# A float32 trunk kernel: the last projection's first 704 tokens by seven products for each two feature tiles, and the convolution's first four products in a written order

## The chip, the cores and the metric

One core of one Trainium2 chip runs the whole program as one launch. The metric is device time in microseconds (us) of one execution, taken as the median of several. TensorE (PE) multiplies, with its weight loads shown apart (PEld); VectorE (DVE), ScalarE (ACT) and GpSimd (POOL) do the elementwise work; SyncE (SP) issues all DMAs.

## The reference, cut to what matters

The reference is a two-layer encoder for 1024 tokens with 1024 features, all in float32. Two stages of it matter here: the gated convolution's input projection, and the second layer's attention into 256 memory tokens with its output projection, behind which only the final norm stands.

```python
def conv_mixer(xn, w_in, conv_w, conv_b, w_out):
    gb, gc, u, gate = jnp.split(xn @ w_in, 4, axis=-1)
    ...

def memory_cross_attention(xn, memn, wq, wkv, wo):
    ...
    o = jnp.einsum('bhsm,bmhd->bshd', p, v).reshape(b, s, D_MODEL)
    return o @ wo

    ...
        x = x + memory_cross_attention(rmsnorm(x, c_norm[i]), rmsnorm(mem, c_mem_norm[i]),
                                       c_wq[i], c_wkv[i], c_wo[i])
    return rmsnorm(x, final_norm)
```

## The kernel before

**Tiling.** Activations lie transposed: eight feature tiles of 128 partitions, each with 1024 tokens. A float32 operand is split into a high part (a cast on ACT, line 214) and a low part (a subtraction on DVE, line 215), and `mm3` multiplies with three matmuls (lines 198 to 200). `dense` makes one feature tile of a projection: 8 input tiles times 3 matmuls for each token part.

**Weights.** `Weights` holds a queue of units in a fixed order (the list `order` at the end of `kernel`). A plain unit is one tile of 1024 columns, split by lines 89 and 90 into two pages, `whi` and `wlo`. A pair entry loads two feature tiles and yields seven units, the left factors A11, S1, A12, S2, S3, S4, A22 of 512 columns each; S1 to S4 are sums and differences that POOL makes (lines 101 to 104; for the first pair DVE makes them), and each factor is split into one page `wf` (lines 113 and 114). There are six pages in all, so the cast of a unit waits until the product with the unit six places ahead is done. Raw weights have two buffers, `wraw`.

**Seven products.** `strassen` multiplies two feature tiles (two by four blocks of 128 input features) with two token halves by seven half-size products in place of eight: left factors times the right factors B11, T1, B21, T2, T3, B22, T4. The convolution's input projection runs so, with 16 pairs of feature tiles and halves of 512 tokens; its right factors are made by `right_factors` while the projection before it runs. `norm_half` for the second token half is issued behind the first pair's first product (`conv_in`).

**The last stages.** `cross` runs four heads; for each, two `dense` calls make the query tiles, then `cross_unit` handles token half 0 and half 1: scores (`pssc`), row maxima (line 851), exponentials (856), normalising (860), transposes (866), and the product with V into `psa`, which goes to an output. For the last head the six output tiles of the earlier heads are split at once (`split_k`), and `last_proj` then runs `dense` over three token parts, 384, 320 and 320 wide, eight feature tiles each. Line 352 adds the old x, `squares` adds up the squares, `norm_soon` makes the norm of a part with two matmuls (lines 286 and 287), and line 360 scales and the result is written out.

**Order.** The program is written in sequence, but a scheduler reorders each engine's instructions by its own timing model; `issue_after` holds instructions back until a named one was issued. Each engine then runs its instructions strictly in the order so fixed, and an instruction whose input is not ready holds up all behind it on its engine.

## Time and profile before

| | us |
|---|---|
| three runs, median (lowest to highest) | 1465.87 (1464.1 to 1466.63) |
| the profiled execution, its own time | 1467.48 |
| span of its trace, first to last instruction | 1465.7 |
| PE busy in the span | 1437.8 (98%) |
| DVE busy, ACT busy, POOL busy | 920.4, 641.4, 259.7 |
| HBM read and written | 124.90 MB and 27.26 MB |

The table's busy times are sums over the span. Matmuls overlap one another in the trace, so a start-to-start distance, not the duration of one, tells what a matmul costs PE. All times below are us from the start of the span.

### The profile page before, as it was taken

The numbers are of one execution on the slowest core, as the hardware profiler recorded it, in microseconds if no ns is written. First come the engines' busy times: TensorE is split into PE (matmuls) and PEld (weight loads), VectorE is DVE, ScalarE is ACT, GpSimd is POOL, SyncE is SP. The second block draws the span as 40 slices with busy tenths as digits, with TensorE's granted clock in tenths as the row PEclk, the third lists the DMA queues.
The fourth block names the chain that finished last, engine by engine and source line by source line (L and its number), as shares of the span: only waits on it lengthen the run. The fifth ranks groups of instructions, "written<-read, shape, count | busy, mean of one in ns | idle before, by whom it ended". The sixth has DMA issues, their size and how long they took to land.

```text
span 1465.7 us, 18632 instructions
## 1 busy us (share of the span) xinstructions
PE 1437.8 (98%) x7128; PEld 1210.9 (83%) x7128; DVE 920.4 (63%) x1368; ACT 641.4 (44%) x1160; POOL 259.7 (18%) x174
## 2 busy tenths in 40 slices
PE   7999999999999999999999999999999999999996
PEld 5888888888888888888887788888888888888996
DVE  7656666677657346446469777777776337446555
ACT  6534653343346244335466533333353325335554
POOL 2300101334220210000112433333310220000221
PEclk9999999999999999999999999999999999999999
DMA  6442223322355421013763111112235532101464
GB/s 218 132 172 71 87 73 101 101 58 72 101 202 193 152 86 44 30 43 130 220 211 119 54 58 58 52 50 58 58 124 188 192 118 79 34 30 40 134 208 152
DMA packets 54216, 157.56 MB, mean 108 GB/s; under 512 B 6640, under 2 KB 17008, under 8 KB 53360
## 3 DMA queue, kind: packets, MB, share of 16 engines
q1 hardware_dynamic: 54128, 156.38, 33.3%
q8 instruction: 56, 0.92, 0.3%
q14 instruction: 32, 0.26, 0.1%
HBM read 124.90 MB, written 27.26 MB: 104 GB/s over the span
## 4 chain that ended last, share of the span: by engine, by line
PE 91%; DVE 4%; DMA 2%; ACT 1%; issue 1%; POOL 0%; SPq 0%; DVEq 0%; ACTq 0%; POOLq 0%
PE psd L198 19%; PE psd L200 19%; PE psd L199 19%; PE pssc L198 6%; PE pssc L199 6%; PE pssc L200 6%; PE psa L199 4%; PE psa L198 4%; PE psa L200 4%; PE pssc L385 1%; DMA wraw<-w_o 1%; PE psa L415 1%; PE psa L866 1%; DVE xnew L360 1%; DVE T L215 0%
## 5 line engine op out<-in xcount | busy, mean ns | idle before, releaser
L198 PE MATMUL psd<-xh,whi 128*128 128x512 f32 (+2 forms) x1096 | 413.4, 381 | 8.8 <-ACT whi L89 7.6
L200 PE MATMUL psd<-xh,wlo 128*128 128x512 f32 (+2 forms) x1096 | 415.3, 380 | 0.9 <-DVE wlo L90 0.9
L199 PE MATMUL psd<-xl,whi 128*128 128x512 f32 (+2 forms) x1096 | 415.9, 380 | 0.0
L198 PEld LDWEIGHTS psd<-xh,whi 128*128 128x128 f32 x1096 | 206.3, 189 | 46.2 <-ACT whi L89 8.5
L200 PEld LDWEIGHTS psd<-xh,wlo 128*128 128x128 f32 x1096 | 206.6, 188 | 36.5 <-DVE wlo L90 1.6
L199 PEld LDWEIGHTS psd<-xl,whi 128*128 128x128 f32 x1096 | 206.6, 189 | 34.0
L89 ACT CAST whi<-wraw 128x1024 fp32r<-128x1024 f32 (+1 forms) x131 | 136.9, 1046 | 204.9 <-PE psd L199 133.9
L90 DVE TENSOR_TENSOR wlo<-wraw,whi 128x1024 fp32r<-128x1024 f32 (+1 forms) x131 | 163.6, 1251 | 71.4 <-ACT whi L89 71.1
L258 POOL TENSOR_TENSOR ssq<-ssq,xold 128x512 f32<-128x512 f32 (+2 forms) x42 | 60.5, 1440 | 415.2 <-ACT xold L256 360.0
L305 DVE TENSOR_TENSOR xnew<-psd,xold 128x512 f32<-128x512 f32 x32 | 21.8, 690 | 93.6 <-PE psd L200 93.6
L113 ACT CAST wf<-ws 128x512 fp32r<-128x512 f32 x64 | 39.6, 622 | 82.2 <-PE pssc L200 33.2
L198 PE MATMUL pssc<-T,wf 128*128 128x512 f32 x192 | 74.8, 390 | 0.6 <-ACT T L214 0.6
L200 PE MATMUL pssc<-T,wf 128*128 128x512 f32 x192 | 74.7, 389 | 0.0
L199 PE MATMUL pssc<-T,wf 128*128 128x512 f32 x192 | 74.7, 389 | 0.0
L258 POOL TENSOR_TENSOR ssq<-ssq,sq 128x512 f32<-128x512 f32 x12 | 19.8, 1650 | 244.6 <-ACT sq L256 244.6
L214 ACT CAST Th<-psa 128x512 fp32r<-128x512 f32 (+1 forms) x62 | 34.5, 590 | 64.2 <-PE psa L415 34.5
L114 DVE TENSOR_TENSOR wf<-ws,wf 128x512 fp32r<-128x512 f32 x64 | 56.0, 877 | 9.8 <-ACT wf L113 8.9
L215 DVE TENSOR_TENSOR Tl<-psa,Th 128x512 fp32r<-128x512 f32 (+1 forms) x62 | 41.7, 687 | 25.9 <-ACT Th L214 25.8
L101 POOL TENSOR_TENSOR ws<-wraw 128x512 f32<-128x512 f32 x15 | 22.1, 1471 | 193.4 <-DMA wraw<-w_o_in 172.4
L292 DVE TENSOR_TENSOR q<-psd,R 128x512 f32<-128x512 f32 x32 | 22.1, 691 | 53.8 <-PE psd L200 53.7
L256 ACT ACTIVATE xold<-xnew 128x512 f32<-128x512 f32 (+2 forms) x49 | 27.7, 567 | 56.2 <-DVE xnew L305 33.4
L113 ACT CAST wf<-wraw 128x512 fp32r<-128x512 f32 x48 | 29.9, 624 | 50.3 <-PE pssc L200 36.9
(316 smaller groups left out, 2997.9 us busy)
## 6 DMA issues: line engine op xcount, KB each, us to landing
wraw<-w_o SPq DMA_DIRECT2D x40, 512.0 KB, 3.8
wraw<-w_o_in SPq DMA_DIRECT2D x32, 512.0 KB, 3.6
wraw<-w_e_in SPq DMA_DIRECT2D x25, 512.0 KB, 3.9
wraw<-w_k SPq DMA_DIRECT2D x16, 512.0 KB, 4.0
mn<-memn SPq DMA_DIRECT2D x16, 512.0 KB, 4.6
wraw<-w_v SPq DMA_DIRECT2D x16, 512.0 KB, 4.6
xold<-x SPq DMA_DIRECT2D x16, 512.0 KB, 5.2
x<-xnew SPq DMA_DIRECT2D x16, 512.0 KB, 2.6
```

The source lines that it names most:

```text
L89: self.nc.scalar.copy(hi[:, c], raw[:, c])
L90: self.nc.vector.tensor_tensor(lo[:, c], raw[:, c], hi[:, c].bitcast(F32), op=ALU.subtract)
L101: tt(F["S1"], F["A21"], F["A22"], op=ALU.add)
L113: self.nc.scalar.copy(hi, src)
L114: self.nc.vector.tensor_tensor(lo, src, hi.bitcast(F32), op=ALU.subtract)
L198: mm(o, ah, bh, start=first, stop=False, skip_group_check=more)
L199: mm(o, ah, bl, start=False, stop=False, skip_group_check=more)
L200: self.last_mm = mm(o, al, bh, start=False, stop=last, skip_group_check=more)
L214: self.nc.scalar.copy(hi, src)
L215: return (eng or self.nc.vector).tensor_tensor(lo, src, hi.bitcast(F32), op=ALU.subtract)
L256: nc.scalar.activation(sq, x, AF.Square)
L258: eng.tensor_tensor(self.ssq[:, a:b], self.ssq[:, a:b], sq, op=ALU.add)
```

## The change

The last projection's first 704 tokens are no longer two dense parts, but four pairs of feature tiles by `strassen` with token halves of 352; the last 320 tokens stay dense. Its right factors are made by the new `last_factors` from the attention's outputs, in two steps: B11, T1 and B21 behind token half 0 of the last head (B21 needs half 0 of that head, tiles 6 and 7), and T2, T3, B22, T4 and the remaining 320 tokens behind half 1 (each of these four needs columns that half 1 writes, for two of its four input tiles). The first pair uses three `psd` banks and its products are issued in written order, behind the last query projection (`last_q`); the later pairs are held back until the first pair's fourth product. The last weights are loaded as four pairs and eight plain tiles, where before each of the eight was loaded three times. The old x comes in pieces of 352 tokens, 16 of them, and 320. The norms of the two halves are issued behind the first and the second of the dense tiles.

In `strassen` the `yield` moves from behind the first product to behind the fourth, and for the convolution's first pair each product's twelve matmuls are issued behind the product before. So `norm_half` of the second token half comes behind the fourth product.

```diff
+    def last_factors(self, x):
+        xh, xl = ([self.buf(tag, "f", dt=F32R) for _ in range(KT)] for tag in ("xh", "xl"))
+        T2, T3 = ([self.buf("e", "f", (P, 4, H), F32R) for _ in range(2)] for _ in range(2))
+        T4 = [self.buf("T", "f", (P, 2, H), F32R) for _ in range(3)]
+        t4 = [self.buf("t", "f", (P, L), F32R) for _ in range(2)]
+        B11, B12, B21, B22 = ([x[4 * i + k][:, j * L : j * L + L] for k in range(4)]
+                              for i in range(2) for j in range(2))
...
+        for k in range(4):
+            split("B11", k, B11[k])
+        for k in range(4):
+            sub(B11[k], B12[k], B11[k])
+            split("T1", k, B11[k])
+        for k in range(4):
+            split("B21", k, B21[k])
+        yield
+        for k in range(4):
+            sub(B11[k], B22[k], B11[k])
+            split("T2", k, B11[k])
+        for k in range(4):
+            sub(B12[k], B22[k], B12[k])
+            split("T3", k, B12[k])
+        for k in range(4):
+            split("B22", k, B22[k])
+        for k in range(4):
+            sub(B21[k], B21[k], B11[k])
+            split("T4", k, B21[k])
+        for k in range(KT):
+            self.split(xh[k][:, 2 * L :], xl[k][:, 2 * L :], x[k][:, 2 * L :])
+        yield out, list(zip(xh, xl))
...
-        for a, b in parts:
             for m in range(KT):
-                old = self.buf("v", "xold", (P, b - a))
-                nc.sync.dma_start(old, x_old[m][:, a:b])
...
+        def pair(p):
+            olds = {(i, j): old(2 * p + i, half[j]) for i, j in ((0, 0), (1, 1), (0, 1), (1, 0))}
+
+            def keep(i, j, ps):
+                t = olds[i, j]
+                nc.vector.tensor_tensor(t, ps, t, op=ALU.add)
+                return t
+
+            def out(i, j, ps, more):
+                added(2 * p + i, half[j], ps, olds[i, j] if more is None else more)
+
+            return self.strassen(B, out, keep, p == 0, L)
+
+        self.last_mm = self.last_q
+        with ExitStack() as behind:
+            for p in range(4):
+                steps = pair(p)
+                next(steps)
+                if p == 0:
+                    first = self.last_mm
+                for _ in steps:
+                    pass
+                if p == 0:
+                    behind.enter_context(self.tc.issue_after(first.ins))
+        c = slice(2 * L, S)
+        for m in range(KT):
+            t = old(m, c)
+            self.dense(ys, lambda a, b, ps: added(m, c, ps, t), ((c.start, c.stop),))
+            if m < 2:
+                with self.tc.issue_after(self.last_mm.ins):
+                    normed(half[1 - m])
+        normed(c)
...
-    def strassen(self, B, out, keep):
+    def strassen(self, B, out, keep, ordered, n=H):
         def product(ps, f, first):
             ah, al = self.w.take()
+            with self.tc.issue_after(self.last_mm.ins) if ordered else ExitStack():
+                four(ps, ah, al, f, first)
...
-        a, c, b = self.ps("sc"), self.ps("a"), self.ps("d")
+        tags = "ddd" if ordered and n < H else ("sc", "a", "d")
+        a, c, b = (self.ps(tag)[:, :n] for tag in tags)
         product(a, "B11", True)
         p1 = keep(0, 0, a)
-        yield
         product(c, "T1", True)
         p5 = keep(1, 1, c)
         product(b, "B21", True)
         out(0, 0, b, p1)
         product(a, "T2", False)
         u2 = keep(0, 1, a)
+        yield
...
-            steps = self.times(B, d, None if i % 2 else AF.Silu)
+            steps = self.times(B, d, None if i % 2 else AF.Silu, i == 0)
...
-    order += mixed("w_o_out", 1, "w_v1", 2) + tiles("w_q1", *["w_o1"] * len(LAST))
+    order += mixed("w_o_out", 1, "w_v1", 2) + tiles("w_q1")
+    o1 = tiles("w_o1")
+    order += [(o1[i], o1[i + 1], W.FACTORS) for i in range(0, len(o1), 2)] + o1
```

**At the start of the convolution, PE.** Names: `pssc_6983`, `psa_6984` and `psd_6985` are the first pair's banks, `pssc_7139`, `psa_7140` and `psd_7141` the second's; T_884 is part of T1, T_907 of T2, T_911 of T3, B_870 of B11 and B_874 of B21. In the program before, `wf_7068`, `wf_7049` and `wf_7085` are S1, A11 and A12 of the second pair, and the order behind the first pair's T2 product is:

```order
L198 MATMUL pssc_6983<-T_907_6898,wf_6908 128x512
L270 MATMUL psa_7009<-sq_928_7007,mean_dr 128x512
L198 MATMUL psa_6984<-T_884_6631,wf_6863 128x512
L199 MATMUL psa_6984<-T_884_6631,wf_6863 128x512
```

The T2 product is cut short by the norm's matmul (line 270), and only then comes the T1 product, 12 matmuls of which two stand here. In the program after, where `wf_7033` and `wf_7085` are the second pair's A11 and A12:

```order
L198 MATMUL pssc_7139<-B_873_6563,wf_7033 128x512
L199 MATMUL pssc_7139<-B_873_6563,wf_7033 128x512
L200 MATMUL pssc_7139<-B_873_6563,wf_7033 128x512
L199 MATMUL pssc_6983<-T_907_6898,wf_6908 128x512
L200 MATMUL pssc_6983<-T_907_6898,wf_6908 128x512
L198 MATMUL psd_7141<-B_874_6566,wf_7085 128x512
L199 MATMUL psd_7141<-B_874_6566,wf_7085 128x512
L198 MATMUL pssc_6983<-T_911_6946,wf_6986 128x512
```

The T1 product now runs ahead of B21 and T2, and the second pair's whole B11 product fills in between T2's matmuls; the norm's matmuls come 20 and 28 rows further on.

**The same place, ACT.** Before:

```order
L214 CAST B_918_6967<-xnew_5953 128x512
L214 CAST sq_928_7007<-ssq_84 128x512
L113 CAST wf_7068<-ws_7043 128x512
L113 CAST wf_7049<-wraw_0_7025 128x512
L701 ACT_TABLE_LOAD
L701 ACTIVATE y_923_6982<-y_923_6982 128x512
L113 CAST wf_7085<-wraw_0_7025 128x512
```

After:

```order
L793 COPY kept_7025<-psa_6984 128x512
L113 CAST wf_7033<-wraw_0_7009 128x512
L214 CAST T_907_6898<-xnew_5949 128x512
L214 CAST T_914_6955<-xnew_5949 128x512
L214 CAST B_915_6958<-xnew_5950 128x512
L214 CAST B_916_6961<-xnew_5951 128x512
L214 CAST B_917_6964<-xnew_5952 128x512
L214 CAST B_918_6967<-xnew_5953 128x512
L113 CAST wf_7052<-ws_7027 128x512
L113 CAST wf_7085<-wraw_0_7009 128x512
L793 COPY kept_7067<-pssc_6983 128x512
L214 CAST sq_932_7070<-ssq_84 128x512
```

The second pair's A11 moves ahead of the last T2 cast; its S1 (from `ws`, which POOL makes) and A12 now stand directly behind the B22 casts, and the table load with the Silu behind them.

**Behind the last head's half 1, PE.** `psa_11121` and `psa_11130` before, `psa_11152` and `psa_11160` after, are that half's products with V. Before:

```order
L199 MATMUL psa_11130<-Tl_11106,V_9221 128x512
L200 MATMUL psa_11130<-Th_11105,V_9222 128x512
L198 MATMUL psd_11259<-xh_10949,whi_11179 128x384
L199 MATMUL psd_11259<-xl_10950,whi_11179 128x384
L198 MATMUL psd_11296<-xh_10949,whi_11216 128x384
```

After, where `f_11053` holds T2 of input tiles 2 and 3, and `f_11036` is B11:

```order
L199 MATMUL psa_11160<-Tl_11137,V_9221 128x512
L200 MATMUL psa_11160<-Th_11136,V_9222 128x512
L198 MATMUL psd_11244<-f_11053,wf_10896 128x352
L199 MATMUL psd_11244<-f_11053,wf_10896 128x352
L200 MATMUL psd_11244<-f_11053,wf_10896 128x352
L198 MATMUL psd_11244<-f_11053,wf_10896 128x352
L199 MATMUL psd_11244<-f_11053,wf_10896 128x352
L200 MATMUL psd_11244<-f_11053,wf_10896 128x352
L198 MATMUL pssc_11386<-f_11036,wf_11286 128x352
```

Before, PE went on with tokens 0 to 383, which are complete; now six matmuls of T2 that need half 1 stand there, and the second pair's products behind them.

**The same place, DVE,** after (before, two subtractions of the outputs stood here, between weight splits). `q_10279`, `q_10280` are input tiles 2 and 3 and `q_10839`, `q_10840` tiles 6 and 7; `x2` marks two rows in one. Between the two pieces stand nine rows of T3, T4 and B22:

```order
L366 TENSOR_TENSOR q_10279<-q_10839,q_10279 128x352 x2
L366 TENSOR_TENSOR q_10839<-q_10839,q_10279 128x352
L366 TENSOR_TENSOR q_10280<-q_10840,q_10280 128x352 x2
L215 TENSOR_TENSOR f_11050<-q_10839,f_11050 128x352
L215 TENSOR_TENSOR f_11050<-q_10839,f_11042 128x320
```

```order
L215 TENSOR_TENSOR f_11051<-q_10840,f_11051 128x352
L215 TENSOR_TENSOR f_11051<-q_10840,f_11043 128x320
L215 TENSOR_TENSOR f_11055<-q_10279,f_11055 128x352
L215 TENSOR_TENSOR f_11058<-q_10839,f_11058 128x352
L215 TENSOR_TENSOR f_11053<-q_10280,f_11053 128x352
L215 TENSOR_TENSOR f_11055<-q_10280,f_11055 128x352
```

The low part of T2's last tile (`f_11053` from `q_10280`) is the sixteenth of DVE's instructions behind half 1's outputs.

## Rows read from the trace of the kernel before

**Rows 1.** The page: the chain's shares by engine; and one line of part 5.

```profile
PE 91%; DVE 4%; DMA 2%; ACT 1%; issue 1%; POOL 0%; SPq 0%; DVEq 0%; ACTq 0%; POOLq 0%
...
L198 PEld LDWEIGHTS psd<-xh,whi 128*128 128x128 f32 x1096 | 206.3, 189 | 46.2 <-ACT whi L89 8.5
```

**Rows 2.** PE's timeline (start, duration, instruction), last stage: scores, and the last matmul.

```profile
1345.14 0.28 PE L198 MATMUL pssc<-K,qh 128*128 128x256 f32 x1
...
1453.69 0.31 PE L200 MATMUL psd<-xh,wlo 128*128 128x320 f32 x1
```

**Rows 3.** PE's timeline: matmuls of 384 columns, 39 apart, and of 320, 56 apart.

```profile
1376.53 0.33 PE L198 MATMUL psd<-xh,whi 128*128 128x384 f32 x1
...
1383.29 0.33 PE L198 MATMUL psd<-xh,whi 128*128 128x384 f32 x1
...
1429.83 0.31 PE L199 MATMUL psd<-xl,whi 128*128 128x320 f32 x1
...
1438.04 0.31 PE L198 MATMUL psd<-xh,whi 128*128 128x320 f32 x1
```

**Rows 4.** Timelines of DVE, ACT and PE: the last head's softmax for half 0.

```profile
1351.14 0.16 DVE L854 TENSOR_SCALAR mx<-mx 128x4 f32<-128x4 f32 x1
...
1353.58 1.14 DVE L860 TENSOR_SCALAR P<-P,sm 128x256 f32<-128x256 f32 x4
...
1357.36 1.04 PE L866 MATMUL psa<-ident,P 128*128 128x128 f32 x8
...
1358.21 1.08 ACT L214 CAST Th<-psa 128x512 fp32r<-128x512 f32 x2 [4.88 <-PE psa L866]
...
1359.28 1.28 DVE L215 TENSOR_TENSOR Tl<-psa,Th 128x512 fp32r<-128x512 f32 x2
```

**Rows 5.** Timelines of DVE and ACT: instructions back to back, of 320, 512 and 384 columns.

```profile
1458.95 3.31 DVE L360 TENSOR_TENSOR xnew<-xnew,R 128x320 f32<-128x320 f32 x8
...
807.23 1.89 DVE L215 TENSOR_TENSOR B<-xnew,B 128x512 fp32r<-128x512 f32 x3
...
1370.00 0.52 ACT L254 ACTIVATE ssq<-xnew 128x384 f32<-128x384 f32 x1
1370.42 0.52 ACT L256 ACTIVATE xold<-xnew 128x384 f32<-128x384 f32 x1
```

**Rows 6.** PE's timeline at the convolution's start; idle time and its cause in brackets.

```profile
797.69 0.39 PE L198 MATMUL psd<-B,wf 128*128 128x512 f32 x1
...
803.20 0.49 PE L198 MATMUL pssc<-T,wf 128*128 128x512 f32 x1 [0.59 <-ACT T L214]
806.40 0.50 PE L270 MATMUL psa<-sq,mean_dr 128*128 128x512 f32 x1 [2.71 <-ACT sq L214]
...
815.74 0.50 PE L198 MATMUL psd<-B,wf 128*128 128x512 f32 x1 [1.49 <-ACT wf L113]
```

**Rows 7.** Windows: length, busy PE, PEld, DVE, ACT, POOL, granted clock, DMA share, GB/s.

```profile
807.65:811.06 3.41, 3.41 (x9) 2.64 (x8) 3.27 (x6) 0.00 (x0) 2.99 (x1) 0.50 0.00 0
...
823.00:1110.00 287.00, 287.00 (x1268) 237.73 (x1267) 216.97 (x268) 109.74 (x178) 79.98 (x56) 1.00 0.23 70
```

**Rows 8.** Timelines of POOL, DVE and ACT around the second pair's sums.

```profile
808.07 3.99 POOL L101 TENSOR_TENSOR ws<-wraw 128x512 f32<-128x512 f32 x1 [9.13 <-DVE B L215]
812.02 1.27 POOL L103 TENSOR_TENSOR ws<-wraw,wraw 128x512 f32<-128x512 f32 x1
...
810.24 0.69 DVE L215 TENSOR_TENSOR sq<-ssq,sq 128x512 fp32r<-128x512 f32 x1
...
812.09 0.62 ACT L113 CAST wf<-ws 128x512 fp32r<-128x512 f32 x1 [5.74 <-POOL ws L101]
812.62 0.62 ACT L113 CAST wf<-wraw 128x512 fp32r<-128x512 f32 x1
```

**Rows 9.** Timelines of POOL and DVE: one overlap where DVE gave way.

```profile
787.88 1.52 POOL L258 TENSOR_TENSOR ssq<-ssq,sq 128x512 f32<-128x512 f32 x1 [5.14 <-ACT sq L256]
...
788.17 1.78 DVE L215 TENSOR_TENSOR T<-xnew,T 128x512 fp32r<-128x512 f32 x1
```

**Rows 10.** SP's timeline, last stage: result writes ahead of a weight load.

```profile
1404.71 4.94 SPq L361 DMA_DIRECT2D out<-xnew  x8
1409.82 0.36 SPq L78 DMA_DIRECT2D wraw<-w_o  x1
```

More of the change, by code (lines that the diff above doesn't have):

```diff
@@ L339, in out_proj_halves, with split, sub @@
         return sq
[L341 to L361 removed]
+    def last_factors(self, x):
[5 more added lines that the diff above has]
+                              for i in range(2) for j in range(2))
+        out = {}
+        def split(f, k, src):
+            if f in ("T2", "T3"):
+                t = (T2 if f == "T2" else T3)[k // 2]
+                hi, lo = t[:, 2 * (k % 2), :L], t[:, 2 * (k % 2) + 1, :L]
+            elif f == "T4":
+                hi, lo = t4 if k == 3 else (T4[k][:, 0, :L], T4[k][:, 1, :L])
+            else:
+                t = (xh if f in ("B11", "T1") else xl)[k + 4 * (f in ("T1", "B22"))]
+                hi, lo = t[:, :L], t[:, L : 2 * L]
+            self.split(hi, lo, src)
+            out.setdefault(f, []).append((hi, lo))
+        def sub(to, a, b):
+            self.nc.vector.tensor_tensor(to, a, b, op=ALU.subtract)
+        for k in range(4):
[20 more added lines that the diff above has]
+        yield out, list(zip(xh, xl))
@@ L712, in out @@
                 nc.vector.tensor_tensor(c, ps, c, op=ALU.mult)
-        return self.strassen(B, out, keep)
+        return self.strassen(B, out, keep, ordered)
     def conv_in(self, B, rest):
@@ L901, in cross @@
             else:
-                ys = [self.split_k(o) for o in wait]
-                ys += [(self.buf("xh", "xh", dt=F32R), self.buf("xl", "xl", dt=F32R))
-                       for _ in range(2)]
-                out = lambda dt, c, ps: self.split(ys[6 + dt][0][:, c], ys[6 + dt][1][:, c], ps)
+                out = lambda dt, c, ps: self.nc.scalar.copy(q[dt][:, c], ps)
+                factors = self.last_factors(wait + q)
             for h in range(2):
                 self.cross_unit(head, h, q, K, V, out)
+                if head == 3 and not paged:
+                    ys = next(factors)
         return ys
```

48 lines of the change are left out of this document (32 added, 16 removed).

## The prediction

> **What bounds the kernel now.** I read the chain of waits first: 91% of it is PE's own work [rows 1], so the kernel is as long as PE's instructions plus the moments in which PE stands still. A change can gain in two ways: fewer columns through PE, or fewer stops. So I read PE's timeline next, at the two places that the change touches, and asked of each stop what ended it; then DVE, ACT and POOL there, since they make what PE will wait for. The sum is made against the profiled execution, 1467.48 us, which is 1.6 above the median of the runs.
>
> What a matmul costs PE: 39 of 384 columns take 6.76 us, 56 of 320 columns 8.21 us [rows 3], so .1733 and .1466 each. 512 columns cost .2263 at the granted clock 1.00 (287.00 us over 1268) [rows 7]. For 352 columns I take the middle of the first two, .160.
>
> **(a) The products.** Removed: the parts of 384 and of 320, 8 x 24 = 192 matmuls each: 192 x .1733 + 192 x .1466 = 61.4 us. Added: 4 pairs x 7 products x 12 = 336 of 352 columns: 336 x .160 = 53.8. The last 320 tokens keep their 192 matmuls (28.1). All lies on PE, so **-7.6**. The weight load lasts 189 ns [rows 1], more than .160, but the 320-column matmuls ran at .1466 beside such loads [rows 3], so it isn't the pace.
>
> **(b) The stops of the last projection before.** From the last head's first score at 1345.14 to the last matmul 1453.69 and its .16 are 108.7 us [rows 2]. PE's work in it: scores 48 x .113 (half of 512 columns), 16 transposes at .13 (1.04 for 8, rows 4), 24 V products x .2263, 89.5 of projection, and at most 12 norm matmuls x .2263: 105.1. So 3.5 us were stops; behind them stand weights that were loaded three times over, and queued on SP behind result writes [rows 10]. After, 8 tiles come as pairs and 8 as plain tiles, instead of 24: I let them all go, **-3.5** (bounds 0 and -3.5).
>
> **(c) The last head's softmax.** New on DVE, between the row maxima and their scaling, are the subtractions of B11, T1 and B21, six of which I count ahead of half 0's scaling. One of 352 columns lies between .40 (320, eight in 3.31) and .605 (512, three in 1.89) [rows 5]: .44. So `mx` comes at 1351.14 + 2.7 = 1353.8, P (1353.58 before) at 1356.3, and the high part of the transposed P, which was cast from 1358.21 on [rows 4], follows behind transposes that P itself paces to about 1357.8. PE meanwhile does scores (1345.14 + 48 x .113 = 1350.6) and 30 of the first pair's matmuls (4.8), and is through at 1355.4. It loses 1.3 us until the transposes are over, .8 until `Th`, .4 at `Tl`: 2.5. For half 1 the same DVE rows are already fewer, but B21's last two input tiles wait for half 0's output: I take 1.9. Together **+4.4**, bounds 2 and 6. Before, PE had 384-column matmuls to put there and lost nothing.
>
> **(d) The stop behind half 1.** This is the largest term. T2's last six matmuls stand right behind half 1's V products, ahead of the second pair's B11 and T1 that would be ready. They need ACT's copy of the output, and then sixteen DVE instructions, fourteen of 352 and two of 320 columns: 14 x .44 + 2 x .40 = 7.0 us. V's end I put at 1369.4 (before, without the waits of c, it would be 1365.0), the copies at 1369.7 and so T2's last low part at 1376.9; a semaphore's way and the cast ahead of it bring 1377.2. PE has only T2's first six matmuls left (6 x .160 = .96) and stands from 1370.3: **+6.9**. POOL's sums for the second pair start in the same stretch. Where POOL and DVE overlap, DVE's subtraction took 1.78 instead of .68 once [rows 9], and POOL's took 3.99 instead of 1.27 another time while DVE went on at its usual pace [rows 8]. Four such sums cost DVE 0 by rows 8 and 4 x 1.1 = 4.4 by rows 9; I take **+1.5**, nearer to rows 8, which show five DVE instructions in a row undisturbed.
>
> **(e) The clock after it.** At 807.65 to 811.06 the granted clock was 0.50, which is 1.2 of the two levels 1.2 and 2.4 GHz, for 3.41 us [rows 7], behind stops that add up to 3.3 us [rows 6]. A stop of 7 us should bring the same: 3.4 us at half pace lose **+1.7** (0; 3.4 if twice).
>
> **(f)** The third pair's sums and its raw weights come just in time, by the order of POOL and SP; **+0.7** (0 to 2). Behind the last matmul stand the same norm and result writes as before: 0.
>
> **(g) The convolution's start.** Before, from the first B21 matmul at 797.69 to the second pair's first B21 matmul at 815.74 are 18.05 us [rows 6] for 42 matmuls (9.5): 8.5 lost, in the stops of .59, 2.71 and 1.49 that the brackets of rows 6 show, two between them, and 1.7 at the low clock. After, 48 matmuls (10.9) stand ahead of that same matmul, since the norm's and T2's come in other places. It waits for the cast of A12, which is behind the cast of S1, which needs POOL's L101 sum, done at 812.06 [rows 8]. DVE's order leaves its instructions back to back to 810.9 as before, so POOL is held as long, and A12 comes at 813.25. PE would be through at 797.69 + 10.9 = 808.6, and stands 4.7 us: 3.8 less than 8.5. Behind so long a stop I expect the low clock again, +1.7. Sum **-2.1** (-6.1 if POOL isn't held and the clock stays; 0 if a second stop appears).
>
> **Sum.** -7.6 - 3.5 + 4.4 + 6.9 + 1.5 + 1.7 + 0.7 - 2.1 = +2.0: 1469.5 against the profiled execution, **1467.9** on the median's scale. Two runs of this kernel can be told apart from about 0.2%, 2.9 us: faster is below 1462.9, slower above 1468.8.
>
> **A rule against the reading in (d) and (g).** What rows 8 show is that POOL was the one held, from 808.07 to 812.06, while DVE started instruction after instruction. The Trainium skill, "SBUF — State Buffer", section "SBUF: two separate sides", says that a DVE instruction with two inputs in SBUF and a GpSimd instruction that reads SBUF share one pair of ports by an exclusive lock, and whoever starts first keeps it for its whole instruction while the other blocks. By that rule POOL, once begun, would not be held over five instructions of DVE; rows 9 agree with it, rows 8 do not. What the other outcome gives is rival 3.
>
> **Rivals.**
> 1. *Slower: POOL takes the factor chain's time.* In (d), each of POOL's four sums holds DVE as in rows 9, 4.4 instead of 1.5, and the longer stop brings a second low-clock stretch. For: DVE's whole chain there reads and writes SBUF. Against: rows 8. It decides once PE's stop behind half 1 is over 8 us. 1467.9 + 2.9 + 1.7 = **1472.5**.
> 2. *Faster: the covers hold.* POOL's L101 at the convolution isn't held (done about 1.5 after its start as in rows 9, so -2.3), the clock stays up there (-1.7) and in the last stage (-1.7), and the softmax costs 2.0, not 4.4. For: the second pair's B11 product is a filler that PE lacked before, and the low clock appeared behind several stops, not one. Against: rows 7 and the order of DVE. 1467.9 - 8.1 = **1459.8**.
> 3. *The first to start keeps its port, everywhere.* The convolution gains 2.3 and 1.7, and the chain of (d) pays 2.9 more: 1467.9 - 1.1 = **1466.8**.
> 4. *The change doesn't do what it says:* 352-column matmuls pace at the weight load's 189 ns, 336 x .029 = +9.7: **1477.6**. Rows 3 speak against it.
>
> **How the numbers follow.** The forecast, that what seven products save is spent on stops, gets .40, with a range of its own from 1463 to 1472 (the bounds of c and d, half each). Rival 1 .22, rival 2 .22, rival 3 .14, rival 4 .02. The forecast's .40 lies .27 within 0.2% and .13 above; rival 3's .14 lies .12 within and .02 below. So faster .22 + .02 = .24, same .39, slower .13 + .22 + .02 = .37. The range runs from 1459.5, which leaves out about half of rival 2, to 1474, which leaves out a quarter of rival 1 and rival 4: some .19.
>
> **What would show it.** Matmuls of 352 columns at .160 from start to start (a). One long stop of PE behind half 1's V products, about 7 us, ended by DVE's line 215 writing T2's last tile (d); if it is under 4, the DVE chain was mis-sized, and the kernel is faster. Transposes of the last head's half 0 waiting for P (c). Granted clock 0.50 just behind that stop, and near 813 (e, g). At the convolution one stop of 4 to 5 us on the cast of A12 in place of several, with POOL's L101 as long as before; if L101 takes 1.5 us, rivals 2 and 3 live. The forecast is wrong above all if ACT or DVE runs the factors in another order of time than I laid them out, so that T2 isn't what PE meets last.

## The result, and the profile after

The changed kernel takes 1473.87 us (median of four runs, 1473.41 to 1474.8), the kernel before 1464.98 beside it: the ratio is 1.0056, with a 95% interval of 1.0041 to 1.0071. It is 8.9 us slower, where the forecast was no change that can be told (1467.9). The time lies inside the range, 6.0 above the forecast and 1.4 above rival 1 (1472.5). The two profiled executions, 1473.89 and 1467.48, are 6.4 apart.

Where the 6.4 are, by the same matmuls in both traces: the convolution's first matmul comes at 794.97 before and 793.47 after, so 1.5 us in favour of the changed kernel stand there already ahead of any part of the change; the last head's first score comes at 1345.14 [rows 2] and 1342.28, so the convolution gives 1.4 more; and from that score to the last matmul are 108.7 us before and 118.0 after: **the last stage is 9.2 us longer.** The chain of waits on the page of the changed kernel answers to [rows 1]:

```profile
PE 89%; DVE 6%; ACT 2%; DMA 1%; POOL 1%; issue 1%; SPq 0%; DVEq 0%; ACTq 0%; POOLq 0%
```

PE's share fell from 91% to 89%, DVE's rose from 4% to 6%. PE's timeline in the last stage after (start, duration, instruction, and in brackets the idle time before it with what ended it):

```profile
1342.28 0.28 PE L198 MATMUL pssc<-K,qh 128*128 128x256 f32 x1
...
1345.16 0.33 PE L198 MATMUL psd<-f,wf 128*128 128x352 f32 x1
...
1349.80 0.32 PE L200 MATMUL psd<-f,wf 128*128 128x352 f32 x1
...
1352.53 0.58 PE L198 MATMUL pssc<-K,qh 128*128 128x256 f32 x1 [2.41 <-ACT P L957]
...
1368.22 0.39 PE L200 MATMUL psa<-Th,V 128*128 128x512 f32 x1
...
1370.91 0.43 PE L198 MATMUL psd<-f,wf 128*128 128x352 f32 x1 [2.31 <-ACT f L214]
1376.83 0.66 PE L199 MATMUL psd<-f,wf 128*128 128x352 f32 x1 [5.49 <-DVE f L215]
...
1379.85 0.66 PE L199 MATMUL psd<-f,wf 128*128 128x352 f32 x1 [1.77 <-DVE f L215]
...
1460.08 0.31 PE L200 MATMUL psd<-f,wlo 128*128 128x320 f32 x1
```

From 1345.16 to 1349.80 are 29 distances, .160 each. Half 1's V products end at 1368.45, and PE goes on with the second pair at 1380.60; between them it did six matmuls. Before, matmuls of 384 columns ran behind those products without a stop, 39 of them in [rows 3]. Windows of the same stretches (length, busy PE, PEld, DVE, ACT, POOL, granted clock, DMA share, GB/s):

```profile
1342.28:1368.45 26.17, 22.54 (x131) 19.92 (x129) 21.40 (x50) 14.56 (x39) 0.00 (x0) 0.93 0.07 21
1368.45:1383.15 14.70, 5.13 (x16) 4.29 (x16) 13.49 (x21) 7.34 (x17) 5.71 (x4) 0.65 0.04 12
1383.15:1460.24 77.09, 76.21 (x481) 74.43 (x481) 52.20 (x79) 42.30 (x76) 33.25 (x26) 1.00 0.52 163
1378.00:1382.00 4.00, 2.23 (x8) 2.16 (x8) 4.00 (x10) 0.62 (x1) 0.00 (x0) 0.50 0.00 0
...
1352.00:1356.00 4.00, 3.47 (x17) 3.48 (x18) 1.84 (x7) 1.39 (x7) 0.00 (x0) 0.57 0.26 103
```

The first stretch holds 20.0 us of PE's work (48 scores x .120, 16 transposes, 24 V products, 42 products x .160), so 6.2 are lost; the second holds 15 x .160 = 2.4 (its sixteenth matmul is the tail of the last V product), so 12.3 are lost; the third holds 75.5 (279 x .160, 28.1 for the last 320 tokens and 2.7 for the norms), so 1.6. Together 20.1 are lost; by the same count, with the scores at .120, the stage before lost 3.3. The work fell by 7.5, where 7.6 was foreseen. DVE is busy for 13.49 us of the second stretch's 14.70. What it did there, and POOL beside it, with the scaling of half 0's row maxima (`mx`) first:

```profile
1351.26 0.16 DVE L955 TENSOR_SCALAR mx<-mx 128x4 f32<-128x4 f32 x1
...
1368.80 6.26 DVE L366 TENSOR_TENSOR q<-q,q 128x352 f32<-128x352 f32 x5 [1.13 <-ACT q L1004]
...
1376.26 3.96 DVE L215 TENSOR_TENSOR f<-q,f 128x352 fp32r<-128x352 f32 x9
...
1368.46 1.26 POOL L101 TENSOR_TENSOR ws<-wraw 128x512 f32<-128x512 f32 x1 [63.88 <-PE psa L199]
...
1372.82 1.43 POOL L104 TENSOR_TENSOR ws<-wraw,ws 128x512 f32<-128x512 f32 x1
```

Five subtractions take 6.26 us while POOL makes its four sums (1368.46 to 1374.25), and nine splits further on, with POOL idle, 3.96: 1.25 each against .44. At the convolution, timelines of PE, POOL and ACT after, for [rows 6, 8]:

```profile
811.90 0.50 PE L198 MATMUL psd<-B,wf 128*128 128x512 f32 x1 [4.04 <-ACT wf L113]
...
806.57 4.11 POOL L101 TENSOR_TENSOR ws<-wraw 128x512 f32<-128x512 f32 x1 [9.00 <-DVE y L799]
...
810.71 0.62 ACT L113 CAST wf<-ws 128x512 fp32r<-128x512 f32 x1 [6.24 <-POOL ws L101]
811.23 0.61 ACT L113 CAST wf<-wraw 128x512 fp32r<-128x512 f32 x1
```

One stop of 4.04 us on the cast of A12 stands in place of several, with POOL's sum as long as before, as forecast.

### The profile page after: what moved, and what is told of

It is laid out like the page before. It is cut to its first block, busy times and chain, and to the rows that moved or that the text cites. A ratio compares the mean times of both kernels' runs of the same rounds, so it can differ in the third digit from the quotient of the medians.

```text
span 1472.1 us, 18631 instructions
## 1 busy us (share of the span) xinstructions
PE 1433.2 (97%) x7080; PEld 1205.2 (82%) x7080; DVE 946.3 (64%) x1434; ACT 647.8 (44%) x1202; POOL 279.7 (19%) x190
## 4 chain that ended last, share of the span: by engine, by line
PE 89%; DVE 6%; ACT 2%; DMA 1%; POOL 1%; issue 1%; SPq 0%; DVEq 0%; ACTq 0%; POOLq 0%
PE psd L198 18%; PE psd L199 18%; PE psd L200 18%; PE pssc L198 6%; PE pssc L199 6%; PE pssc L200 6%; PE psa L199 4%; PE psa L198 4%; PE psa L200 4%; PE pssc L481 1%; PE psa L511 1%; DVE f L215 1%; PE psa L967 1%; DVE q L366 1%; DVE wf L114 1%
## 5 line engine op out<-in xcount | busy, mean ns | idle before, releaser
L198 PE MATMUL psd<-xh,whi 128*128 128x512 f32 x904 | 351.6, 393 | 8.3 <-ACT whi L89 7.5
L200 PE MATMUL psd<-xh,wlo 128*128 128x512 f32 x904 | 353.8, 392 | 0.2 <-DVE wlo L90 0.2
L199 PE MATMUL psd<-xl,whi 128*128 128x512 f32 x904 | 353.9, 392 | 0.0
L198 PEld LDWEIGHTS psd<-xh,whi 128*128 128x128 f32 x904 | 170.2, 188 | 44.7 <-ACT whi L89 8.1
L89 ACT CAST whi<-wraw 128x1024 fp32r<-128x1024 f32 (+1 forms) x115 | 120.0, 1044 | 180.1 <-PE psd L199 119.3
L200 PEld LDWEIGHTS psd<-xh,wlo 128*128 128x128 f32 x904 | 170.1, 188 | 34.9 <-DVE wlo L90 0.6
L199 PEld LDWEIGHTS psd<-xl,whi 128*128 128x128 f32 x904 | 170.2, 188 | 33.7 <-DVE xl L227 0.3
L90 DVE TENSOR_TENSOR wlo<-wraw,whi 128x1024 fp32r<-128x1024 f32 (+1 forms) x115 | 143.8, 1253 | 52.3 <-ACT whi L89 52.1
L101 POOL TENSOR_TENSOR ws<-wraw 128x512 f32<-128x512 f32 x19 | 27.3, 1436 | 352.1 <-DMA wraw<-w_o_in 146.8
L258 POOL TENSOR_TENSOR ssq<-ssq,xold 128x512 f32<-128x512 f32 x24 | 36.7, 1528 | 197.0 <-ACT xold L256 137.3
L198 PE MATMUL psd<-y,whi 128*128 128x512 f32 x128 | 50.0, 391 | 0.0
```

The source lines that it names most:

```text
L89: self.nc.scalar.copy(hi[:, c], raw[:, c])
L90: self.nc.vector.tensor_tensor(lo[:, c], raw[:, c], hi[:, c].bitcast(F32), op=ALU.subtract)
L101: tt(F["S1"], F["A21"], F["A22"], op=ALU.add)
L198: mm(o, ah, bh, start=first, stop=False, skip_group_check=more)
L199: mm(o, ah, bl, start=False, stop=False, skip_group_check=more)
L200: self.last_mm = mm(o, al, bh, start=False, stop=last, skip_group_check=more)
```

## The experiments

**The theory and its rivals.** Theory: the last stage lost what seven products save, and more, because T2 is the sixteenth instruction of DVE behind half 1 and POOL's sums hold DVE there. Rivals: the two parts of the change interact; the sums cost nothing that counts; the stop only changes its place when it is attacked. All ratios below are against the kernel before, in runs on the same chip.

**The two parts apart.** e1 is the kernel before with the changed `strassen` for the convolution; e2 is the changed kernel without it:

```diff
         p1 = keep(0, 0, a)
+        if not ordered:
+            yield
...
-        yield
+        if ordered:
+            yield
...
-            steps = self.times(B, d, None if i % 2 else AF.Silu, i == 0)
+            steps = self.times(B, d, None if i % 2 else AF.Silu)
```

> The kernel before with the convolution's part of the change alone: the first four products of the first pair in written order, the second half's norm behind the fourth. Theory: the two traces differ by -1.5 us already in the first 10 us of the program, which is no part of the change; from there to the last head the convolution takes the shift from -1.5 to -2.9, so this kernel is 1.4 us faster than the one before (1463.6 against 1465.0), and the stop on the cast of A12 is there as in the whole change, about 4 us long with a stretch of half clock behind it. Rival: the gain is given back by the time the attention starts, and the kernel is within 0.5 us of before. A rival of the opposite sort, that my forecast's -2.1 is the size and the trace was a poor execution, would show 1462.9 or less.

> The whole change without the convolution's part: the last projection by seven products, the convolution's first pair unordered with the norm behind its first product as before. Theory: the last stage alone is longer by 9.2 us (from the last head's first score to the last matmul 118.0 us in the changed kernel, 108.7 before), so this kernel takes 1474 to 1475.5, which is 1.4 slower than the whole change. Rival: the two parts meet somewhere (weights prefetched across them), and this kernel is as fast as the whole change, 1473.9, or slower than 1476.5.

e1: 1463.32, ratio 0.9989 (0.9980 to 0.9997). The convolution's part gains 1.7 us. e2: 1476.56, ratio 1.0077 (1.0064 to 1.0089). The last projection's part costs 11.5, one more than expected. The parts add up to 9.8, beside 8.9 for the whole. e2's six times fall into two groups: 1473.9 to 1474.99, as expected, and 1478.14 to 1479.31. Its trace is of the upper group, and has a second low clock behind two short stops (.46 and .79 us), which the whole change doesn't have there (windows of e2, then of the changed kernel). That this is what parts the two groups one trace can't show:

```profile
1416.00:1420.00 4.00, 3.75 (x14) 3.75 (x15) 3.22 (x5) 0.66 (x2) 4.00 (x3) 0.57 0.08 12
```

```profile
1416.00:1420.00 4.00, 4.00 (x27) 4.00 (x26) 2.21 (x4) 3.42 (x7) 3.44 (x4) 1.00 0.69 205
```

**POOL's sums, moved ahead.**

```diff
-            s13, s24 = self.sums(), self.sums()
+            tag = "v" if i == len(self.order) - 11 else "T"
+            s13, s24 = self.sums(tag), self.sums(tag)
...
-        xs = [self.buf("v" if m < 4 else "r", "xnew") for m in range(KT)]
+        xs = [self.buf("v" if m < 2 else "r", "xnew") for m in range(KT)]
```

> The whole change, with one buffer choice altered: the four sums that POOL makes for the last projection's second pair go to buffers that the last head's queries leave, so that POOL can make them while the softmax of half 1 runs, not while DVE makes T2. DVE's order of the T2 chain stays word for word, with one split ahead of it. Theory: POOL's sums, which start first, hold DVE for most of each of them; without them the five subtractions behind half 1 take 5 x .44 = 2.2 us and not 6.26, T2's last low part comes 4 us earlier, and the kernel takes 1469 to 1470 (4 to 5 less than 1473.9, the half clock behind the stop may stay). Rival A: the chain of sixteen DVE instructions with its casts is itself the length, POOL took little of it: the five subtractions stay above 5 us or the gain is under 1 us. Rival B: the sums hold DVE in the softmax instead and the stop is only moved: the scaling of P in half 1 later by 3 us, the time 1473 to 1474.

e3: 1473.11, ratio 1.0056 (1.0044 to 1.0068): rival B. DVE's timeline of e3, its window behind the stop at half 1's scores, two short stops of PE later on, and the window behind them:

```profile
1354.47 2.18 DVE L962 TENSOR_SCALAR P<-P,sm 128x256 f32<-128x256 f32 x4
...
1357.77 1.63 DVE L216 TENSOR_TENSOR f<-q,f 128x352 fp32r<-128x352 f32 x1
1359.32 1.22 DVE L956 TENSOR_SCALAR mx<-mx 128x4 f32<-128x4 f32 x1
...
1372.57 2.27 DVE L367 TENSOR_TENSOR q<-q,q 128x352 f32<-128x352 f32 x5 [0.54 <-ACT q L1005]
...
1353.36 0.39 PE L199 MATMUL pssc<-K,qh 128*128 128x256 f32 x1 [2.40 <-ACT P L958]
...
1354.00:1356.00 2.00, 2.00 (x19) 2.00 (x19) 1.71 (x5) 0.22 (x2) 0.84 (x1) 1.00 0.12 47
...
1411.48 0.43 PE L199 MATMUL psa<-f,wf 128*128 128x352 f32 x1 [0.90 <-ACT wf L114]
1414.31 0.43 PE L201 MATMUL pssc<-f,wf 128*128 128x352 f32 x1 [0.79 <-DVE wf L115]
...
1416.00:1420.00 4.00, 4.00 (x27) 4.00 (x26) 2.96 (x5) 2.76 (x6) 3.69 (x4) 1.00 0.57 159
```

The five subtractions take 2.27 instead of 6.26, so it was POOL that held them: 4.0 us. But POOL now works from 1355.15 to 1360.51, and there P's scaling takes 2.18 instead of 1.14, a split 1.63 and the scaling of four numbers a partition 1.22 instead of .16. The five subtractions start 3.77 us later than in the changed kernel (.84 of it stands already at the first score), and PE's last wait for T2 ends at 1379.62, beside 1379.85.

**T2 first on DVE.** The subtractions and splits of T3, B22, T4 and of the last 320 tokens of tiles 6 and 7 are held until T2's last low part is issued:

```diff
         for k in range(4):
             sub(B11[k], B22[k], B11[k])
-            split("T2", k, B11[k])
+            t2 = split("T2", k, B11[k])
...
+        with self.tc.issue_after(t2.ins):
+            for k in range(4):
+                sub(B12[k], B22[k], B12[k])
+                split("T3", k, B12[k])
...
```

> The whole change, with the rest of the factors (T3, B22, T4, the last 320 tokens of tiles 6 and 7) held behind T2's last low part on DVE and ACT: T2's low part is the fourth DVE instruction behind half 1's output, not the sixteenth. POOL's sums stay where they are. Theory: four instructions at the 1.25 us that they took beside POOL's sums are 5 us after 1368.8, so T2 is ready at 1374 and not at 1379.8, and the kernel takes 1468 to 1469 (5 to 6 less); the stop on T2 stays, some 4 us. Rival A: T3, B22 and T4 come too late for the first pair's last three products, which follow 36 matmuls (5.8 us) later, a second stop takes the place of the first, and the gain is under 2 us. Rival B: the stop isn't T2's place in DVE's order but the copies of half 1's output on ACT and the cast ahead of each split: gain under 1.5 us.

e4: 1468.80, ratio 1.0027 (1.0016 to 1.0039): 5.1 less than the changed kernel, as expected. PE's timeline of e4, and DVE's:

```profile
1350.38 0.39 PE L198 MATMUL pssc<-K,qh 128*128 128x256 f32 x1 [0.67 <-ACT P L960]
...
1367.62 0.43 PE L198 MATMUL psd<-f,wf 128*128 128x352 f32 x1 [2.57 <-ACT f L214]
1369.62 0.66 PE L199 MATMUL psd<-f,wf 128*128 128x352 f32 x1 [1.57 <-DVE f L215]
1371.13 0.66 PE L199 MATMUL psd<-f,wf 128*128 128x352 f32 x1 [0.26 <-DVE f L215]
...
1377.39 0.43 PE L198 MATMUL psa<-f,wf 128*128 128x352 f32 x1 [1.73 <-ACT wf L113]
...
1348.65 0.17 DVE L958 TENSOR_SCALAR mx<-mx 128x4 f32<-128x4 f32 x1
...
1365.24 2.82 DVE L366 TENSOR_TENSOR q<-q,q 128x352 f32<-128x352 f32 x2 [1.98 <-ACT q L1007]
1367.98 3.09 DVE L215 TENSOR_TENSOR f<-q,f 128x352 fp32r<-128x352 f32 x2
```

From the last V product to T2's last stop it takes 6.5 us instead of 11.6, with POOL's sums still beside the four instructions (5.8 us for what is 1.8 alone). So T2's place among DVE's instructions cost 5.1 there, more than POOL's 4.0. But that isn't where the whole gain comes from, and the agreement with the expectation is partly luck. The hold also clears DVE ahead of half 0's softmax: `mx` comes 6.8 us behind the first score instead of 9.0, PE's stop at half 1's scores is .67 instead of 2.41, no low clock follows it, and from the first score to the end of the V products are 23.0 us instead of 26.2. Behind T2 3.3 are given back, in a new stop of 1.73 on the cast of S1 with a second low clock behind it (0.57 from 1378 to 1382): 5.1 and 3.2 less, 3.3 more, 5.0 in the trace.

**Then the sums behind T2, and a filler.** e5 adds to e4 that POOL writes one column from T2's last low part into S1's buffer ahead of S1, so that its sums wait for T2. e6 adds to e5 that the later pairs are held only until the first pair's third product.

```diff
+            if i == len(self.order) - 11:
+                tt(F["S1"][:, :1], self.t2, self.t2, op=ALU.add)
             tt(F["S1"], F["A21"], F["A22"], op=ALU.add)
...
         product(b, "B21", True)
+        self.third = self.last_mm
...
-                    first = self.last_mm
+                    first = self.third
```

> The kernel with T2 first (1468.8), and POOL's four sums for the second pair held until T2's last low part is written: POOL adds one column of it into the buffer of S1 before it makes S1, which S1 then overwrites. Theory: DVE's four instructions for T2 then run without POOL beside them, 4 x .44 = 1.8 us instead of the 5.8 from 1365.24 to 1371.07, T2 is ready 3.5 to 4 us earlier, and no DVE instruction that anyone waits for meets the sums. S1 is written about 2.5 us later than now, so the stop on the cast of S1 (1.7 us at 1377.4) may grow by 1 to 2: 1465.5 to 1467.5. Rival: the sums only change their victim once more, as they did when they were made early (the stop moved to the softmax and 0.8 us was left): S1 or T3 is late by what T2 gains, and the time stays at 1468 to 1469.

> The same as e5, and the second pair's products are held back only until the first pair's third product (B21), not its fourth (T2), so that its B11 and B21 products (24 matmuls, 3.8 us) can run while T2 is being made. Theory: the stop behind half 1, which has 2.5 us left for the copy and the cast and some 1.8 for DVE, is filled, another 2 to 3 us less than e5, 1463 to 1465, and no half clock behind it. Rival: what PE does early it then lacks later, because the second pair's T1 needs S1, which POOL now makes late: a stop on S1's cast of the same size appears and e6 is within 1 us of e5.

e5: 1472.45, ratio 1.0053 (1.0040 to 1.0066), 3.7 *more* than e4, 2.1 of it between the first score and the last matmul of the two traces. e6: 1471.68, ratio 1.0047 (1.0033 to 1.0060). Both theories failed. PE's and DVE's timelines of e5:

```profile
1381.65 0.66 PE L200 MATMUL psd<-f,wf 128*128 128x352 f32 x1 [6.78 <-DVE xold L437]
...
1369.41 0.96 DVE L217 TENSOR_TENSOR f<-q,f 128x352 fp32r<-128x352 f32 x2 [1.34 <-ACT f L216]
1370.29 4.00 DVE L368 TENSOR_TENSOR q<-q,q 128x352 f32<-128x352 f32 x4
1374.21 3.97 DVE L217 TENSOR_TENSOR f<-q,f 128x352 fp32r<-128x352 f32 x4
1378.10 1.82 DVE L368 TENSOR_TENSOR q<-q,q 128x352 f32<-128x352 f32 x4
...
1381.08 0.51 DVE L437 TENSOR_TENSOR xold<-psd,xold 128x352 f32<-128x352 f32 x1
```

T2 is ready at 1370.3, and DVE's splits of it, .96 for two, met no POOL. But the eight instructions behind them now meet it: 4.00 + 3.97 where four subtractions alone take 1.82. The addition that empties T2's bank (line 437 here) stands sixteenth behind T2 on DVE, and T3's matmuls, which need that bank, stand on PE ahead of the rest of the second pair's B21 and of its T1 in this order. So PE stops for 6.78 us there. In e6 the same stop is 9.83 us: the filler was used up earlier, and nothing was left for this place. Three places were tried for the sums, ahead of T2, beside it and behind it, and each time DVE paid for them: 3.2 us (the excess of the three groups in e3), 4.0 and 4.3.

**The sums left out.** S1 to S4 of the second pair are replaced by plain blocks of the weights, so the second pair's output isn't the projection's; the work of PE, ACT and DVE stays.

> The whole change with the second pair's four sums left out of the last projection (plain blocks of the weights stand in for S1 to S4, so the output of that pair is not the projection). DVE's chain for T2 stays in its order. Theory: made late or early, the four sums take about 4 us from DVE on the path to PE's next work; without them nothing pays: 4 to 5 us less than 1473.9, 1469 to 1470, the five subtractions behind half 1 at 2.2 us and P's scaling of half 0 at 1.14. Rival: POOL's sums cost the path nothing, as their early making showed (1473.1): 1473 or more; the 0.8 us would then be their whole price.

e11: 1474.26, ratio 1.0056 (1.0044 to 1.0068). The expected 4 us did not come out at the end. They were there: against the changed kernel the matmuls at 1383.5 come 4.1 us earlier, and at 1403 still 4.1. (The first score stands .95 later in e11, and the low clock at half 1's scores, 1.4 us of the changed kernel's first stretch, is missing.) Then (PE's timeline and a window of e11):

```profile
1408.14 0.43 PE L200 MATMUL psa<-f,wf 128*128 128x352 f32 x1 [1.27 <-ACT wf L115]
1410.96 0.66 PE L202 MATMUL pssc<-f,wf 128*128 128x352 f32 x1 [0.78 <-DVE wf L116]
```

```profile
1412.00:1416.00 4.00, 4.00 (x15) 4.00 (x15) 1.95 (x3) 0.00 (x0) 2.74 (x2) 0.50 0.40 107
```

The fourth pair's S1 is only 2.5 us earlier, since POOL starts it when its raw weights land (1406.17 against 1408.72): a stop of 1.27, which with one of .78 (the changed kernel has .79 there) was followed by the low clock, 2.7 us more lost by 1417. So what POOL holds DVE is real, and yet it isn't shown that the kernel would be faster without it. Whether a version without the later stop would keep the 4 us was not tried.

**Work for PE during the softmax.** Half 1's query matmuls of the last head (48 of 512 columns) go behind half 0's scores (e7; its new `queries` multiplies one token half); e8 is e7, e5 and e6's hold together.

```diff
+            late = head == 3 and not paged
+            if late:
+                self.w.prepare()
+                for dt in range(2):
+                    queries(dt, self.w.used + dt, 0)
...
                 self.cross_unit(head, h, q, K, V, out)
+                if late and h == 0:
+                    for dt in range(2):
+                        queries(dt, self.w.used, 1)
+                        self.w.take()
```

> The whole change, and the last head's queries of token half 1 (48 matmuls of 512 columns, 10.9 us) are computed behind half 0's scores instead of ahead of them, so that PE has work that waits for nothing during half 0's softmax. Theory: between the last head's first score and the end of half 1's V products PE lost about 6 us (26.2 us for 20.0 of work; the forecast had 4.4); with the queries there it loses 1 to 2, and the kernel takes 1469 to 1470 (4 to 5 less than 1473.9). The stop on T2 stays, about as long as before, 10 to 12 us with its half clock. Rival A: the factors B11, T1 and B21 then stand in half 1's softmax, DVE is late there instead, and under 1.5 us is gained. Rival B: the late queries take the weight pages, the first pair's factors are split late, and the time is over 1474.

> All of it together: the whole change with T2 first, POOL's sums behind T2, the second pair held only until the third product, and half 1's queries behind half 0's scores. Theory: the losses are separate stops of one engine and add up: 1473.9 - 5.1 (T2 first, measured) - 3 (sums late) - 1.5 (fill) - 4.5 (queries) = 1460, which is 5 us faster than the kernel before and 3 less than the convolution's part alone (1463.3). Then the saving of the seven products, 7.6 us, is what is left when PE isn't made to wait. Rival: some other limit (the wraw loads, SP behind the result writes, DVE with 97 of the last 140 us) takes over: 1463 to 1466, with a new stop in the later pairs.

e7: 1483.62, ratio 1.0127 (1.0113 to 1.0141), the slowest of all. e8: 1478.34, ratio 1.0091 (1.0078 to 1.0105). PE's timeline of e7, and a window:

```profile
1369.63 1.94 PE L967 MATMUL psa<-ident,P 128*128 128x128 f32 x8 [3.88 <-DVE P L961]
...
1385.31 0.66 PE L199 MATMUL psd<-f,wf 128*128 128x352 f32 x1 [5.29 <-DVE f L215]
...
1388.76 0.66 PE L199 MATMUL psd<-f,wf 128*128 128x352 f32 x1 [2.21 <-DVE f L215]
```

```profile
1366.00:1392.00 26.00, 12.34 (x35) 9.53 (x36) 17.67 (x33) 12.07 (x30) 5.72 (x4) 0.58 0.02 8
```

This is the run that told me most. The queries did fill half 0's softmax, but they are the start of half 1's own chain: queries, scores, maxima, exponentials, scaling, transposes, V, copy, factors. Begun later, it ends later, and by then all other work is used up. From half 1's last row maximum on DVE to PE's last wait for T2 is a train of small steps, 22.7 us long in the changed kernel (1357.11 to 1379.85), 17.6 in e4 and 25.7 in e7, and in e7 PE had little to do beside it: it was busy 12.34 of 26 us at a mean clock of 0.58.

**Factors that need no half 1.** With halves of 256 tokens no factor reads half 1; 512 tokens stay dense.

```diff
-L = 352
+L = 256
...
             split("B21", k, B21[k])
-        yield
...
+        yield
         for k in range(KT):
             self.split(xh[k][:, 2 * L :], xl[k][:, 2 * L :], x[k][:, 2 * L :])
...
```

> The whole change with halves of 256 tokens instead of 352: the first 512 tokens by seven products, 512 tokens dense, and all seven factors made behind half 0 of the last head, since none reads half 1 any more. Saved on PE against the kernel before: 89.6 - (336 x .120, the distance of the 256-column scores, + 192 x .2263 = 83.8) = 5.8 us instead of 7.6. Theory: what ate the saving is that T2, T3, B22 and T4 wait for half 1 while DVE is PE's only source of work; here the stop behind half 1 of 10 to 12 us is gone, and the dense last part is wider, which makes the end longer by about 3 us (8 x .2 on DVE and longer writes). 1473.9 - 11 + 1.8 + 3 = 1467 or better, 1461 to 1467. Rival: DVE, which now makes all factors between the two softmaxes, holds the softmax of half 1 back by as much: 1470 or more.

e10: 1482.70, ratio 1.0114 (1.0101 to 1.0127). The theory, that it is half 1 alone that comes late, fell. DVE's timeline of e10:

```profile
1378.68 5.77 DVE L215 TENSOR_TENSOR f<-q,f 128x256 fp32r<-128x256 f32 x5 [2.76 <-ACT f L214]
```

From its first score (1342.84) to the end of its last projection matmul (1466.02) are 123.2 us for 99.8 of work (336 x .120 + 192 x .2263 = 83.8, and 16.0 for the rest): 23.4 lost, more than in the changed kernel. B21, T2, T3, B22 and T4 still need half 0 of the same head, and T3's casts and splits, which need nothing of half 1, stand on ACT and DVE behind the steps of half 1's softmax, where POOL's sums then meet them (5.77 us for five). The longer end was as expected: 15.4 us from the first norm matmul to the end of the span, against 11.9.

**The convolution's stop.** In every pair B21 with A12 goes ahead of T1 with S1, so that ACT's cast of A12 doesn't stand behind that of S1; on top of e1 (e9) and of e10 (e12).

```diff
-    FACTORS = ("A11", "S1", "A12", "S2", "S3", "S4", "A22")
+    FACTORS = ("A11", "A12", "S1", "S2", "S3", "S4", "A22")
```

> The convolution's part alone (1463.3), and in every pair the third product (B21 with A12) before the second (T1 with S1), with the weight pages in that order. In the convolution's second pair ACT then casts A12, which is a raw block, ahead of S1, which waits for POOL. Theory: the stop of 4 us in the whole change and in the convolution's part alone is A12 standing behind S1 on ACT, and S1 behind POOL's sum, which DVE holds for 4 us; with A12 first PE goes on with 24 matmuls of T3 and B22 (5.4 us) before it needs S1, so the stop and the half clock behind it (1.7) go: 1458 to 1460. Rival: DVE is late with T3's and B22's low parts in this stretch, so the stop only changes its name: 1462 or more.

> e10 with the order of products of e9, in the convolution and in the last projection. Theory: the two are hundreds of us apart and add up: e10 less what e9 gains over the convolution's part alone (3 to 5 us); if e10 is near 1462 this one is near 1458 and faster than every other. Rival: in the last projection the changed order asks for B21 earlier than DVE has it, and gives 1 to 3 us back there.

e9: 1464.83, ratio 0.9998 (0.9989 to 1.0007); e12: 1483.25, ratio 1.0120 (1.0107 to 1.0133). No gain in either. PE's and ACT's timelines of e9:

```profile
811.80 0.50 PE L198 MATMUL pssc<-T,wf 128*128 128x512 f32 x1 [3.61 <-ACT kept L697]
...
810.64 0.62 ACT L113 CAST wf<-ws 128x512 fp32r<-128x512 f32 x1 [5.84 <-POOL ws L101]
811.17 0.58 ACT L697 COPY kept<-pssc 128x512 f32<-128x512 f32 x1
```

A12 was cast early, but now the copy that empties T2's bank stands behind the cast of S1 on ACT, and T3 waits for that bank: 3.61 us in place of 4.09. In both it is the instruction that stands second on ACT, behind the cast of S1, that PE waits for.

No version that keeps the new last projection came down to the kernel before; e4 is the nearest, 0.27% above it. The convolution's part alone, e1, has the lowest ratio of all that ran, though its interval reaches to 0.9997.

## Why the prediction was right or wrong, point by point

The time was inside the range, but the forecast's balance of saving and stops did not hold: the stops won by 6 us. By the traces the sum was short by 1.8 at (c), 2.2 at (d) and (e), 1.1 at (b) with (f) and .7 at (g). All four lie on the same side, so that the time still fell below 1474 is owed to the width of the range and not to the sum. I had given *slower* .37 and *same* .39.

- **(a) products, -7.6.** Right: .160 a matmul, -7.5.
- **(b) stops of the stage before, -3.5.** One stop on weights was left, .79 at 1413.55 (DVE's line 114), which is (f)'s .7; the whole rest of the stage behind 1383 lost 1.6. The scores cost .120 each, not .113, so the stage before lost 3.3, and (b) with (f) gained 1.7 where I had 2.8.
- **(c) softmax, +4.4.** Measured 6.2. The step on DVE held: from the first score to `mx` 6.0 us before [rows 2, 4] and 9.0 after (1351.26), 3.0 later against my 2.7. The step on PE failed: I had PE wait at the transposes, and it stopped earlier, 2.41 us at half 1's scores, which need the `pssc` banks that half 0's exponentials still read. Before, PE lost nothing there, for it had the 384-column matmuls. And a low clock (0.57) followed that stop, for which I had nothing; behind a stop of 2.40 at the same place e3 kept 1.00, so some 1.4 of the 6.2 are this execution's.
- **(d) the stop behind half 1, +6.9 and +1.5.** The place, its cause and its end were right (DVE's line 215 on T2's last tile); the size of POOL's share was the term that was mis-sized: 4.0 us (e3 against the changed kernel), where I took 1.5 by [rows 8]. [Rows 9], the other end of my bounds, were the ones that fitted: POOL came first there, as it did here.
- **(e) clock, +1.7.** It came as described, at 0.50 behind the stop; (d), (e) and POOL together are 12.3 against 10.1.
- **(g) the convolution, -2.1.** -1.4 in the traces, -1.7 by e1. POOL was held 4.11 us as forecast, the stop was 4.04 against 4.7, and the low clock came (0.50 from 813.20 to 816.30).
- **The rivals.** Rival 1 named half of what is seen, POOL holding DVE for about four times 1.0, and a time 1.4 off. The second low clock that it set behind the longer stop isn't there: the other stretch, at 0.57, lies ahead of that stop, behind half 0's softmax. So the nearness of its time is partly luck. Its price was not borne out as a price at the end: without the sums (e11) the kernel is as slow. Rival 3's price for the chain was right too, but its gain at the convolution wasn't there, for POOL was held as before. Rival 2 fell.

What the runs put in place of my sum: I priced each stop by itself, as if it could be filled or shortened alone. In the runs the stops hang together. Before, tokens 0 to 383 gave PE 33.3 us of matmuls (192 x .1733) that needed no half 1. Of the seven right factors four need it, and in this kernel's order PE has only the first pair's first three products ahead of them; what follows waits for one train of small steps through DVE and ACT. Beginning that train later cost some 10 us (e7). Clearing DVE for it gained 5.1 (e4), in half 0's softmax as well as behind half 1. Moving POOL's sums or PE's filler to another place gained nothing (e3 against the changed kernel, e5 and e6 against e4).

Two things are only argued. One is that the saving would come out whole if the train were short enough. The other is that the four factors are the cause, and not the order: the first three products of every pair need no half 1 (4 x 36 x .160 = 23.0 us), but the later pairs are held behind the first pair's fourth product. e6 loosened this for the second pair, and the stop moved to T2's bank; an order with more of these products ahead of T2 was not tried.

## What to carry to other kernels

Before you cut a matrix product by mixing its operands, count how much work is left that doesn't need the operand that comes last, and set it against the length of the chain that makes that operand; multiplications saved behind such a chain need not be time saved. When a stop is found, ask what the instruction behind it in the same queue waits for next: here most attempts only moved a stop, from T2 to its bank, from the cast of S1 to a copy, from behind the softmax into it, and in the last stage only the one that shortened the chain itself gained. Test the parts of a change apart: the small one (the convolution's order, -1.7 us, just clear of the noise) gained, and it was hidden under the large one.

## What the runs showed of the hardware

- **DVE and POOL: who comes first, and who comes next.** At the convolution DVE runs back to back and POOL's L101 begins at 806.57 and is held over five DVE instructions, the last of which ends at 809.55; it is done at 810.68. So POOL didn't get in between two instructions of DVE. In the last stage POOL runs its four sums back to back, and DVE does get in: about one instruction of DVE passes with each sum (5 in 6.26 us, 4 in 4.00). The Trainium skill, "SBUF — State Buffer", section "SBUF: two separate sides", says that whoever starts first keeps the shared pair for its whole instruction; the second case agrees, with 1.25 us for a subtraction that takes .44 alone, and for the first the section doesn't say who of two waiting engines is next. In both cases here it was DVE.
- **Instructions with a single tensor as input are held too:** the scaling of P (four in 2.18 instead of 1.14) and of `mx`, four numbers a partition (1.22 instead of .16), in e3.
- **Short stops and the clock.** A stop of .79 us at 1413.55 left the granted clock at 1.00 in the changed kernel. With a stop of .46 ahead of it (e2) the window behind it was at 0.57, and with 1.27 (e11) at 0.50, the lower of the two levels, 1.2 GHz; but with .90 (e3) it stayed at 1.00. In the same way the stop at half 1's scores, 2.41 in the changed kernel and 2.40 in e3, was followed by 0.57 in the one and by 1.00 in the other. So in these traces the length of the stops doesn't tell whether the clock falls; where it fell, a small second stop cost more than itself (2.7 us in e11).
